# First norm's modulation in pieces of 128 columns, x turned by diagonal matmuls, and a 23rd weight slot that the second gate uses later

## The chip, the cores and the metric

The kernel runs on one core of a Trainium2 chip. The metric is the device time of one execution in microseconds (us). The core has a matmul engine (TensorE, "PE" in the profile, whose weight loads are listed apart as "PEld"), two elementwise engines (VectorE, "DVE", and ScalarE, "ACT"), GpSimd ("POOL"), a queue engine ("SP") and 16 DMA engines. Each engine works through its own list of instructions in the order of the program. Engines wait for one another through semaphores. TensorE's clock has two levels, and the profile shows which was granted (1.00 is 2.4 GHz, 0.50 is 1.2 GHz).

## The reference

One transformer block on 256 tokens of width 1024, everything in float32. What matters here:

```
mod = silu(c) @ w_ada + b_ada                     # 6 x 1024
sh1, sc1, ga1, sh2, sc2, ga2 = split(mod)
h = rms_norm(x, g_norm1) * (1 + sc1) + sh1
z = h @ w_in                                      # q, k, v, conv parts, gates
merged = gate_a * (attention @ w_pa) + gate_b * (conv @ w_pb)
x = x + ga1 * (merged @ w_o)
h2 = rms_norm(x, g_norm2) * (1 + sc2) + sh2
x = x + ga2 * moe(h2)      # top group of 4, top 2 of 8 experts, 32 experts, SwiGLU, width 512
```

## The kernel before

All weights pass once through the core, about 257 MB, as one stream of DMAs of 1 MB (768 KB for the pieces of q, k, v), laid out on the host in the order of use. `stream` lists them: first the 54 pieces of `FRONT` (w_ada, w_in, w_pa, w_pb, w_o), then for each of 8 groups of four experts 16 pieces of w1 and w3 and 8 of w2, 192 in all. A piece goes into a slot (1 MB of SBUF). `pump` issues the next piece from SP whenever a slot is free, and `release`, called where a piece was last read, frees its slot and calls `pump`. Slots and order are settled when the program is built; on the chip SP waits at each issue for the semaphore that says that the slot's last reader is done, and for its eighth DMA back to have landed. There are 12 slots at first, two more lent by the gate buffers, and as buffers of the front are given up `more_slots` adds 3 (`late`), 4 (`late2`) and 3 (`late3`), while the lent ones go: 22 slots in the expert stage.

**The front** is a list of units. A unit takes 512 columns of a weight, splits them into a high and a low part (ACT L396 and DVE or POOL L397, up to four units ahead), and does three fp32r matmuls for each product on PE (L428). There are 24 units for q, k, v (three for each of 8 row blocks k), 56 for the other columns of w_in, 16 for w_pa and w_pb, and 16 for w_o. Other work is put between units as tasks: `after(i, g)` starts task g behind unit i, and each `yield n` lets n units pass.

**The first norm's modulation** must be there before the units of row block k: `hpart(0, k)` and `hpart(1, k)` (high and low part of h, transposed) are made by `modulate1(k)` from hf (x, normed and transposed), a1 (1 + scale, times g_norm1) and sh1. The scale and the shift come as four pieces of 256 columns each, two row blocks to a piece, in the order of the list `FIRST`. A piece is summed over its 1024 rows either by 8 matmuls of 32x256 on PE (L516) followed by two small ones that turn the row into columns (L501), or, for the scale pieces 2 and 3, by 8 operations on DVE (L331, L333) and the same two small matmuls. At the start x is multiplied by its 1/rms (DVE L360, ACT L361) and turned by 16 PE transposes (L365). The copies L372 and L374 bring it back to SBUF as hf.

**The second gate** ga2 is summed in the front into bank B[0] (`gate2_task`, L773). It is copied to `ysb` after the front, and finished between the first group's `up` and `down` with its bias row, which ACT loads at L937.

**The end of the front.** After the last unit of w_o the residual, the squares, the transposes and the router's logits (L844) follow, then a chain of small DVE operations picks the experts up to the one-hot `ohs` (L980). PE ranks the tokens (L982 to L984), DVE makes the gather matrices Gt and Wt (L1016, L1018), PE gathers tokens with `gather` (L1027), DVE and ACT modulate them with `modulate2`, and `up(0)` begins its matmuls (L1060). Nothing of the expert weights is released before that. `warm(n)` is n matmuls of ident by ident (L267) whose result nobody reads; they only keep PE busy.

## Time and profile before

| | us |
|---|---|
| median of 3 runs | 663.52 (663.48 to 663.66) |
| the profiled execution | 665.23 |
| its span, first to last instruction | 663.5 |
| PE busy | 533.8 |
| DVE busy | 195.5 |
| ACT busy | 146.7 |

Busy times are sums over stages with different limits, and PE's ends are modelled, so a PE that waits inside a run of matmuls can be shown as busy. HBM reads are 257.12 MB, 389 GB/s over the span. The chain that ended last has 34% of the span in DMA and 3% in PE; it is followed back only as far as 410.71 us.

### The profile page before, as it was taken

Reading aid. Unit: us, or ns where it says so; the run is one execution under the profiler, and the core shown is the slowest. Engines: PE = TensorE matmul, PEld = TensorE weight load, DVE = VectorE, ACT = ScalarE, POOL = GpSimd, SP = SyncE. Lnnn points to the kernel's source line nnn. Section 1 sums busy time; section 2 is a strip of 40 time slices with the busy share of each in tenths; the row PEclk is TensorE's granted clock in tenths of the full one; section 3 lists DMA queues with packets and bytes.
Section 4 is the critical chain, followed back from the end, with each engine's and each line's share of the span. In section 5 each row is a group of like instructions: output and inputs, shape, how many; then the busy total and the mean of one; then the engine's idle time right before and its main releaser. Section 6 shows DMA issues by size and latency. Waiting matters only on the chain. (4 is left out here: it accounts for less than half of the span.)

```text
span 663.5 us, 11736 instructions
## 1 busy us (share of the span) xinstructions
PE 533.8 (80%) x5054; PEld 322.1 (49%) x5055; DVE 195.5 (29%) x405; ACT 146.7 (22%) x290; POOL 40.9 (6%) x59
## 2 busy tenths in 40 slices
PE   7999999999999899988575756676766875677765
PEld 6678897988998637363043104301510540161033
DVE  4687449657896412020020001001100100010002
ACT  4536456744555220010010001000000100010001
POOL 0012511500040000000000000000000000000000
PEclk9999999999999898999888799968987596897669
DMA  8999994699959699999999997999999999999996
GB/s 315 426 425 398 426 421 154 244 356 378 399 199 407 282 410 426 425 427 424 428 427 423 423 426 328 423 428 427 425 426 426 428 426 425 428 425 425 427 427 255
DMA packets 37765, 259.01 MB, mean 390 GB/s; under 512 B 4545, under 2 KB 5673, under 8 KB 7242
## 3 DMA queue, kind: packets, MB, share of 16 engines
q1 hardware_dynamic: 36136, 256.98, 93.4%
q10 hardware_dynamic: 1362, 1.05, 0.5%
q8 instruction: 42, 0.69, 0.4%
q0 software_dynamic: 208, 0.15, 0.1%
q14 instruction: 17, 0.14, 0.1%
HBM read 257.12 MB, written 1.05 MB: 389 GB/s over the span
## 5 line engine op out<-in xcount | busy, mean ns | idle before, releaser
L1060 PE MATMUL ps<-slot,xg 128*32 128x512 f32 x1024 | 163.4, 745 | 76.4 <-DMA slot<-in_up_dram 71.4
L1060 PEld LDWEIGHTS ps<-slot,xg 128*32 128x32 f32 x1024 | 26.1, 120 | 197.8 <-DMA slot<-in_up_dram 160.3
L428 PE MATMUL ps<-hbuf,sthi 128*128 128x256 f32 x512 | 94.8, 287 | 0.0
L428 PEld LDWEIGHTS ps<-hbuf,sthi 128*128 128x128 f32 x512 | 79.0, 190 | 11.4 <-ACT sthi L396 6.7
L397 DVE TENSOR_TENSOR stlo<-slot,sthi 128x512 fp32r<-128x512 f32 x100 | 72.0, 723 | 37.9 <-ACT sthi L396 36.7
L396 ACT ACTIVATE sthi<-slot 128x512 fp32r<-128x512 f32 x108 | 68.0, 630 | 62.7 <-PE ps L428 50.2
L1068 DVE TENSOR_TENSOR sl<-sl,ps 128x512 f32<-128x512 f32 x8 | 5.5, 688 | 254.7 <-PE ps L1060 246.4
L1080 PE MATMUL ps<-slot,sl 128*32 128x128 f32 x2048 | 67.9, 287 | 14.6 <-DMA slot<-in_down_dram 9.7
L428 PE MATMUL ps<-hbuf,stlo 128*128 128x256 f32 x256 | 72.2, 282 | 0.7 <-POOL stlo L397 0.7
L1080 PEld LDWEIGHTS ps<-slot,sl 128*32 128x32 f32 x2048 | 57.1, 115 | 29.1 <-DMA slot<-in_down_dram 13.3
L1047 ACT ACTIVATE GW<-ps 128x256 f32<-128x256 f32 x8 | 3.1, 384 | 239.1 <-PE ps L1046 239.1
L1088 PE MATMUL ps<-ysb,GW 128*128 128x512 f32 (+1 forms) x76 | 37.1, 615 | 17.6 <-DVE ysb L1086 17.6
L428 PEld LDWEIGHTS ps<-hbuf,stlo 128*128 128x128 f32 x256 | 48.5, 190 | 0.9 <-POOL stlo L397 0.9
L428 PE MATMUL ps<-sthi,hbuf 128*128 128x512 f32 x128 | 43.2, 404 | 1.1 <-ACT hbuf L528 0.9
L1086 DVE TENSOR_TENSOR ysb<-ps,ga 128x512 f32<-128x512 f32 (+1 forms) x19 | 11.5, 606 | 90.7 <-PE ps L1080 83.7
L1027 PEld LDWEIGHTS ps<-GW,x 128*128 128x128 f32 x256 | 33.4, 212 | 6.4 <-issue 5.6
L1027 PE MATMUL ps<-GW,x 128*128 128x128 f32 x256 | 36.0, 302 | 0.2 <-DVE GW L1018 0.2
L1088 PEld LDWEIGHTS ps<-ysb,GW 128*128 128x128 f32 x76 | 13.3, 203 | 30.9 <-DVE ysb L1086 22.1
L428 PEld LDWEIGHTS ps<-sthi,hbuf 128*128 128x128 f32 x128 | 23.7, 188 | 8.9 <-issue 1.6
L1033 ACT ACTIVATE xg<-ps,sm,sm 128x128 f32<-128x128 f32 x32 | 12.4, 457 | 59.8 <-PE ps L1027 59.8
L428 PE MATMUL ps<-stlo,hbuf 128*128 128x512 f32 x64 | 25.1, 392 | 0.0
L1035 DVE TENSOR_SCALAR xg<-ps,sm,sm 128x128 f32<-128x128 f32 x32 | 11.2, 404 | 35.0 <-PE ps L1027 35.0
(264 smaller groups left out, 429.2 us busy)
## 6 DMA issues: line engine op xcount, KB each, us to landing
slot<-in_up_dram SPq DMA_DIRECT2D x128, 1024.0 KB, 19.6
slot<-in_down_dram SPq DMA_DIRECT2D x64, 1024.0 KB, 19.6
slot<-in_front_dram SPq DMA_DIRECT2D x42, 1024.0 KB, 11.4
slot<-in_front_dram SPq DMA_DIRECT2D x8, 768.0 KB, 14.4
gates<-in_front_dram SPq DMA_DIRECT2D x4, 1024.0 KB, 7.0
x<-in_x_dram SPq DMA_DIRECT2D x2, 512.0 KB, 3.7
out_dram<-x ACTq DMA_DIRECT2D x1, 512.0 KB
out_dram<-x ACTq DMA_DIRECT2D x4, 128.0 KB, 1.8
```

The source lines that it names most:

```text
L396: S.activation(hi, src, AF.Copy)
L397: (G if i in on_pool else V).tensor_sub(lo, src, hi.bitcast(F32))
L428: PE.matmul(o, l, r, start=start and n == 0, stop=stop and n == 2, skip_group_check=True)
L1027: PE.matmul(o[:, 128 * (k % 4):128 * (k % 4) + 128], x[:, t, 128 * k:128 * k + 128], Gt[:, t, :], start=t == 0, stop=t == 1)
L1033: S.activation(xg[:, k, :], src, AF.Identity, bias=sh2[:, k:k + 1], scale=a2[:, k:k + 1])
L1035: V.tensor_scalar(xg[:, k, :], src, a2[:, k:k + 1], sh2[:, k:k + 1], op0=OP.mult, op1=OP.add)
L1047: S.activation(WT.rearrange("p t n -> p (t n)"), YC[:, :256], AF.Copy)
L1060: PE.matmul(o[js, :], xg[:, k, js], w[:, j, :], start=k == 0, stop=k == DK - 1)
L1068: V.tensor_mul(sl, sl, HB)
L1080: PE.matmul(bank[js, cs], hidT[:, k, js], w[:, 4 * j + k, :], start=k == 0, stop=k == 3, skip_group_check=True)
L1086: V.tensor_mul(ysb[:, cs], (bank or (YC, YD)[n])[:, cs], ga2[:, ns])
L1088: PE.matmul(ACC[t][n][:, cs], WT[:, t, :], ysb[:, cs], start=q == 0, stop=q == NQ - 1, skip_group_check=True)
```

## The change

- `FIRST` goes. The scale and the shift now come as 8 pieces `mod1.i` of 1 MB, each with the 128 scale and the 128 shift columns of row block i, in turn with `qkv.i`. Every piece is summed on PE (8 matmuls of 32x256), copied by DVE, turned by two small matmuls, and a1 and sh1 of that block are made by one DVE operation each. Task i starts behind unit 3i - 3.
- c, b_ada and g_norm1 are loaded from ACT's queue instead of SP's. x is now first on SP, and four pieces follow it before the other small loads.
- x is not scaled first: two diagonal matrices (ident times 1/rms) are made, and `x_turn(b)` does x times diagonal as ordinary matmuls, four to a bank.
- `late3` has 4 slots instead of 3: 23 in all, until the piece w3.0.7 is used up. Its slot is then kept (`kept`) and holds ga2 and ysb.
- The bias row of ga2 is loaded by ACT into misc in the front, and added in bank B[0] by two matmuls with one row, ahead of the first sums of `gate2_task`, which starts two units earlier and lets two units pass. The copy of B[0] to ysb moves behind `up(0)`.
- Around the router: `squares(1, 1)` and the sums for 1/rms move up; `warm(8)` becomes `warm(26)`, `warm(4)` becomes `warm(9)`; two blocks of tokens instead of three are gathered before the first matmuls of `up(0)`; the transposes of Wt come one step later.

```diff
-    for nm in FIRST:
-        i = int(nm[2:])
-        if nm[0] == "q":
-            f.append((f"qkv.{i}", "w_in", 128 * i, 1, 0, 1536))
-        else:
-            f.append((f"{nm[:2]}1.{i}", "w_ada", 0, 8, 512 * (SC1 if nm[:2] == "sc" else SH1) + 256 * i, 256))
+    for i in range(DK):
+        f.append((f"mod1.{i}", "mod1", 0, 8, 256 * i, 256))
+        f.append((f"qkv.{i}", "w_in", 128 * i, 1, 0, 1536))
...
     def release(key):
-        free.append(where.pop(key))
+        i = where.pop(key)
+        if key == LAST_UP:
+            kept.append(i)
+            return
+        free.append(i)
         pump()
...
-    load_rows("c", SY)
+    load_rows("c", S)
+    load_rows("b_ada", S)
+    load_rows("g_norm1", S)
...
-    load_rows("b_ada", SY)
-    load_rows("g_norm1", SY)
-    pump(1)
+    pump(4)
     for nm in ("g_norm2", "conv_w", "conv_b"):
         load_rows(nm, SY)
-    pump(2)
...
-    xh = [flat(sq), flat(vt)]
-    V.tensor_scalar(xh[0], x[:, 0, :], rinv1[:, 0:1], None, op0=OP.mult)
-    S.activation(xh[1], x[:, 1, :], AF.Copy, scale=rinv1[:, 1:2])
-
-    def x_transposes(t):
-        for k in range(DK):
-            PE.transpose(PS[k // 2][:, 256 * (k % 2) + 128 * t:256 * (k % 2) + 128 * t + 128],
-                         xh[t][:, 128 * k:128 * k + 128], ident)
-
-    def x_copies():
...
+    dg = flat(sq)[:, :256].rearrange("p (t n) -> p t n", t=2)
+    for t in range(2):
+        V.tensor_scalar(dg[:, t], ident, rinv1[:, t:t + 1], None, op0=OP.mult)
+
+    def x_turn(b):
+
+        for k in (2 * b, 2 * b + 1):
+            for t in range(2):
+                PE.matmul(PS[b][:, 256 * (k % 2) + 128 * t:256 * (k % 2) + 128 * t + 128],
+                          x[:, t, 128 * k:128 * k + 128], dg[:, t], start=True, stop=True)
+        d = flat(hf[:, 2 * b:2 * b + 2, :])
+        if b % 2:
+            S.activation(d, PS[b], AF.Copy)
+        else:
+            V.tensor_copy(d, PS[b])
...
-    def first_ada(i, shift, bank):
-
-        key = f"{('sc', 'sh')[shift]}1.{i}"
-        w = cols256(slot(key))
+    ab1 = small([128, 8])
+
+    def first_bias():
+
+        V.scalar_tensor_tensor(ab1, col("b_ada", 4 * SC1, 8), 1.0, col("g_norm1", 0, 8), op0=OP.add, op1=OP.mult)
+
+    def first_ada(i):
+
+        bank = B[6 + i % 2]
+        w = cols256(slot(f"mod1.{i}"))
         for kk in range(2):
             for j in range(4):
-                k = 2 * j + kk
+                k = 4 * kk + j
                 PE.matmul(bank[32 * j:32 * j + 32, :256], sil[:, k:k + 1].to_broadcast([128, 32]), w[:, k, :],
                           start=kk == 0, stop=kk == 1)
-        release(key)
-        p = part[shift][:, :256]
-        if shift and not i:
-            V.tensor_copy(p, bank[:, :256])
-        else:
-            S.activation(p, bank[:, :256], AF.Copy)
-        yield 1
-        first_cols(i, shift, bank, p, sel)
+        release(f"mod1.{i}")
+        p = part[i % 2][:, :256]
+        V.tensor_copy(p, bank[:, :256])
+        yield 1
+        for c in range(2):
+            PE.matmul(bank[:, c:c + 1], p[:, 128 * c:128 * c + 128], sel, start=True, stop=True)
+        V.scalar_tensor_tensor(a1[:, i:i + 1], bank[:, 0:1], col("g_norm1", i, 1), ab1[:, i:i + 1], op0=OP.mult,
+                               op1=OP.add)
+        V.tensor_add(sh1[:, i:i + 1], bank[:, 1:2], col("b_ada", 4 * SH1 + i, 1))
+
+    def first_task(i):
+        yield from first_ada(i)
+        modulate1(i)
...
-    def first_scale(i):
-
...
-        p = misc[:, 256 * i:256 * i + 256]
-        w = cols256(slot(f"sc1.{i}"))
-        for k in range(DK):
-            ada_sum(p, w[:, k, :], k, k == 0)
-            if k % 2:
-                yield 1
-        release(f"sc1.{i}")
-        first_cols(i, 0, B[6], p, one)
-
-    def first_shift(i):
-
-        yield from first_ada(i, 1, B[7])
-        for k in (2 * i, 2 * i + 1):
-            modulate1(k)
-            yield 1
...
     def gate2_task(bank):
 
+        row = misc[0:1, :D]
+        S.dma_start(row, dram("b_ada", 512 * GA2, [[D, 1], [1, D]]))
+        yield 2
+        for half in range(2):
+            PE.matmul(bank[64 * half:64 * half + 32, :], one[0:1, :].to_broadcast([1, 32]),
+                      row[:, 512 * half:512 * half + 512], start=True, stop=False, skip_group_check=True)
         for i in range(4):
             for kk in range(2):
                 for half in range(2):
-                    quarter_sum(f"ga2.{i}", 2 * i + kk, 2 * kk + half, 2 * half + kk, bank, i == 0, i == 3)
+                    quarter_sum(f"ga2.{i}", 2 * i + kk, 2 * kk + half, 2 * half + kk, bank, i == 0 and kk == 1, i == 3)
             release(f"ga2.{i}")
             yield 3
...
-    for i in range(1, 4):
-        after(6 * i - 6, lambda i=i: first_scale(i))
-        after(6 * i - 3, lambda i=i: first_shift(i))
+    for i in range(1, DK):
+        after(3 * i - 3, lambda i=i: first_task(i))
...
-    after(63, lambda: gate2_task(B[0]))
+    after(61, lambda: gate2_task(B[0]))
...
-    a, b = first_ada(0, 0, B[6]), first_ada(0, 1, B[7])
+    first = first_ada(0)
     columns("a", B[4])
-    next(a)
-    x_transposes(0)
-    next(a, 0)
-    x_transposes(1)
-    x_copies()
-    next(b)
-    warm(4)
-    next(b, 0)
-    for k in range(2):
-        split_next()
-        modulate1(k)
-    run_units(19)
+    first_bias()
+    x_turn(0)
+    next(first)
+    for b in range(1, 4):
+        x_turn(b)
+    split_next()
+    next(first, 0)
+    modulate1(0)
+    run_units(20)
...
-    more_slots(late3, 3)
+    more_slots(late3, 4)
...
-    ysb = late3.tile([128, 512], F32, name="ysb")
...
-    ga2 = late3.tile([128, D], F32, name="ga2")
     small_pool[0] = late3
-    S.dma_start(ga2[0:1, :], dram("b_ada", 512 * GA2, [[D, 1], [1, D]]))
...
     resid(1, 1)
     for t in range(2):
         logits(0, t)
+    squares(1, 1)
+    ms2, rinv2, nu2 = small([128, 2]), small([128, 2]), small([128, 2])
+    V.tensor_add(ms2, ss2[:, :, 0], ss2[:, :, 1])
+    V.tensor_scalar(ms2, ms2, 1.0 / D, EPS, op0=OP.mult, op1=OP.add)
     transp(1, 0)
-    squares(1, 1)
+    S.activation(rinv2, ms2, AF.Sqrt)
     transp(1, 1)
     for t in range(2):
         logits(1, t)
-    S.activation(ysb, B[0], AF.Copy)
-    warm(8, B[4])
-
-    ms2, rinv2, nu2 = small([128, 2]), small([128, 2]), small([128, 2])
-    V.tensor_add(ms2, ss2[:, :, 0], ss2[:, :, 1])
-    V.tensor_scalar(ms2, ms2, 1.0 / D, EPS, op0=OP.mult, op1=OP.add)
-    S.activation(rinv2, ms2, AF.Sqrt)
+    warm(26, B[4])
...
-    warm(4, B[4])
+    warm(9, B[4])
...
             if q == 0:
 
-                for kk in range(min(k + 2, DK) if k else 0, min(k + 3, DK)):
+                for kk in range(k + 1 if k else 0, min(k + 2, DK)):
...
-            if k == (6 if q == 0 else 4):
+            if k == (7 if q == 0 else 4):
                 weights_T(q)
...
     for q in range(NQ):
         up(q)
         if q == 0:
+            room = flat(slots[kept[0]])
+            ga2, ysb = room[:, :D], room[:, D:D + 512]
+            S.activation(ysb, B[0], AF.Copy)
             for half in range(2):
-                g = ga2[:, 512 * half:512 * half + 512]
-                PE.matmul((HA, HB)[half], sel2[:, half:half + 1].to_broadcast([128, 128]), ysb, start=True, stop=False)
-                PE.matmul((HA, HB)[half], one[0:1, :].to_broadcast([1, 128]), g[0:1, :], start=False, stop=True)
-                V.tensor_copy(g, (HA, HB)[half])
+                PE.matmul((HA, HB)[half], sel2[:, half:half + 1].to_broadcast([128, 128]), ysb, start=True, stop=True)
+                V.tensor_copy(ga2[:, 512 * half:512 * half + 512], (HA, HB)[half])
...
+    w["mod1"] = np.stack([w["w_ada"][:, 512 * b:512 * b + D].reshape(D, DK, 128) for b in (SC1, SH1)], 2).reshape(D, -1)
```

In PE's list at the end of the front, from the clock matmuls behind the router's logits to the first expert matmuls (ps_74 and ps_73 are the bank that nobody reads, sm_2222 and sm_2244 the one-hots `ohs`, GW the gather matrices, and a slot with xg an expert matmul), before:

```order
L267 MATMUL ps_74<-ident 128x128 x8
L982 LDWEIGHTS before
L982 MATMUL ps_73<-sm_2222,before 128x32
L983 LDWEIGHTS ones
L983 MATMUL ps_73<-sm_2222,ones 128x32
L984 LDWEIGHTS before
L984 MATMUL ps_73<-sm_2222,before 128x32
L267 MATMUL ps_74<-ident 128x128 x4
L1027 MATMUL ps_76<-GW,x 128x128 x2
L1027 MATMUL ps_77<-GW,x 128x128 x2
L1027 MATMUL ps_76<-GW,x 128x128 x2
L1060 MATMUL ps_74<-slot_1526,xg 32x512 x4
```

and now:

```order
L265 MATMUL ps_73<-ident 128x128 x26
L957 LDWEIGHTS before
L957 MATMUL ps_72<-sm_2244,before 128x32
L958 LDWEIGHTS ones
L958 MATMUL ps_72<-sm_2244,ones 128x32
L959 LDWEIGHTS before
L959 MATMUL ps_72<-sm_2244,before 128x32
L265 MATMUL ps_73<-ident 128x128 x9
L1002 MATMUL ps_75<-GW,x 128x128 x2
L1002 MATMUL ps_76<-GW,x 128x128 x2
L1035 MATMUL ps_73<-slot_1532,xg 32x512 x4
```

The ranking matmuls stand behind 26 clock matmuls instead of 8, the gathers behind 9 instead of 4, and the expert matmuls behind two gathered blocks instead of three.

In DVE's list at the start, from the end of 1/rms to the modulation of the first row block (ps_70 to ps_73 are the banks with x turned, gates_114 is hf, sm_221 is a1, sm_222 is sh1, stlo and sthi are the parts of the first unit's weights), before:

```order
L323 SCALAR_TENSOR_TENSOR sm_227<-sm_228,sm_227 128x2
L360 TENSOR_SCALAR sq<-x,sm_227 128x1024
L257 COPY cols_a<-ps_74 128x56
L506 TENSOR_TENSOR sm_221<-ps_76,cols_a 128x2
L507 SCALAR_TENSOR_TENSOR sm_221<-sm_221,cols_a 128x2
L374 COPY gates_114<-ps_70 128x512
L374 COPY gates_114<-ps_72 128x512
L521 COPY part_220<-ps_77 128x256
L504 TENSOR_TENSOR sm_222<-ps_77,cols_a 128x2
L397 TENSOR_TENSOR stlo_105<-slot_79,sthi_101 128x512
L529 TENSOR_SCALAR gates_114<-gates_114,sm_221,sm_222 128x256
L530 TENSOR_TENSOR hbuf_99<-gates_114,hbuf_99 128x256
```

and now (hf is gates_113, a1 is sm_220, sh1 is sm_221, the banks are ps_69 to ps_72):

```order
L321 SCALAR_TENSOR_TENSOR sm_226<-sm_227,sm_226 128x2
L359 TENSOR_SCALAR sq<-ident,sm_226 128x128 x2
L255 COPY cols_a<-ps_73 128x56
L500 SCALAR_TENSOR_TENSOR sm_238<-cols_a 128x8
L371 COPY gates_113<-ps_69 128x512
L513 COPY part_218<-ps_75 128x256
L371 COPY gates_113<-ps_71 128x512
L394 TENSOR_TENSOR stlo_104<-slot_77,sthi_100 128x512
L517 SCALAR_TENSOR_TENSOR sm_220<-ps_75,cols_a,sm_238 128x1
L519 TENSOR_TENSOR sm_221<-ps_75,cols_a 128x1
L527 TENSOR_SCALAR gates_113<-gates_113,sm_220,sm_221 128x256
L528 TENSOR_TENSOR hbuf_98<-gates_113,hbuf_98 128x256
```

a1 and sh1 of the first row block, which the modulation waits for, now stand behind the split L394 of the first unit's weights; before, L397 stood behind them.

## Rows read from the trace of the kernel before

**Rows 1.** The page, the span in 40 slices of 16.6 us: DMA's rate.

```profile
GB/s 315 426 425 398 426 421 154 244 356 378 399 199 407 282 410 426 425 427 424 428 427 423 423 426 328 423 428 427 425 426 426 428 426 425 428 425 425 427 427 255
```

**Rows 2.** Waits of PE, 24 to 205 us: waited for, us in total, times, longest.

```profile
PE ps L773 <- DVE sq L642: 1.0, 1, 1.0
PE ps L428 <- POOL stlo L397: 0.7, 1, 0.7
```

**Rows 3.** Timeline of the start: start, us, engine, line, output<-input, count, idle before.

```profile
0.78 0.41 SPq L224 DMA_DIRECT2D qkb<-in_c_dram  x1
1.24 0.83 SPq L229 DMA_DIRECT2D x<-in_x_dram  x2
...
8.56 0.16 DVE L323 SCALAR_TENSOR_TENSOR sm<-sm,sm 128x2 f32<-128x2 f32 x1
...
11.04 1.09 PE L365 MATMUL ps<-ident,sq 128*128 128x128 f32 x8
...
15.49 0.63 ACT L396 ACTIVATE sthi<-slot 128x512 fp32r<-128x512 f32 x1 [1.39 <-DMA slot<-in_front_dram]
...
15.87 0.16 DVE L504 TENSOR_TENSOR sm<-ps,cols_a 128x2 f32<-128x2 f32 x1 [0.95 <-PE ps L501]
16.06 0.60 ACT L528 ACTIVATE hbuf<-gates,sm,sm 128x256 fp32r<-128x256 f32 x1
16.15 0.69 DVE L397 TENSOR_TENSOR stlo<-slot,sthi 128x512 fp32r<-128x512 f32 x1
...
16.72 0.50 PE L428 MATMUL ps<-sthi,hbuf 128*128 128x512 f32 x1 [0.89 <-ACT hbuf L528]
```

**Rows 4.** Timeline of PE among the units of q, k, v, around 27 and 46 us.

```profile
26.89 0.39 PE L428 MATMUL ps<-sthi,hbuf 128*128 128x512 f32 x1
27.12 0.50 PE L501 MATMUL ps<-sel,part 128*128 128x1 f32 x4
27.48 0.48 PE L428 MATMUL ps<-sthi,hbuf 128*128 128x512 f32 x1
...
45.79 0.40 PE L428 MATMUL ps<-sthi,hbuf 128*128 128x512 f32 x1
46.11 1.07 PE L516 MATMUL ps<-gates,sm 128*32 128x256 f32 x16
47.11 0.50 PE L428 MATMUL ps<-sthi,hbuf 128*128 128x512 f32 x1
```

**Rows 5.** Timeline where the second gate's sums begin, and the issue of its bias row.

```profile
133.01 0.60 ACT L694 ACTIVATE qkb<-ps 128x512 f32<-128x512 f32 x1 [2.01 <-PE ps L691]
...
136.44 1.06 PE L773 MATMUL ps<-slot,sm 128*32 128x512 f32 x8
...
215.10 0.52 ACTq L937 DMA_DIRECT2D ga<-in_b_ada_dram  x1
```

**Rows 6.** Waits of SP's queue, 210 to 232 us.

```profile
SPq L137 <- DMA ga<-in_b_ada_dram: 4.2, 1, 4.2
```

**Rows 7.** Timeline from the router's last logits to the first expert matmuls.

```profile
219.01 2.03 PE L267 MATMUL ps<-ident 128*128 128x128 f32 x16
...
222.41 0.23 DVE L980 TENSOR_TENSOR sm<-sm 128x64 bf16<-128x64 f32 x1
222.69 0.18 PE L982 MATMUL ps<-sm,before 128*128 128x32 bf16 x1 [1.64 <-DVE sm L980]
...
223.66 0.42 DVE L1018 TENSOR_TENSOR GW<-GW,sm 128x256 f32<-128x256 f32 x1
224.14 2.48 PEld L1027 LDWEIGHTS ps<-GW,x 128*128 128x128 f32 x12 [0.43 <-DVE GW L1018]
...
226.84 2.36 PE L1060 MATMUL ps<-slot,xg 128*32 128x512 f32 x16
...
229.13 0.71 PE L1027 MATMUL ps<-GW,x 128*128 128x128 f32 x4
```

**Rows 8.** Timeline of SP: the two issues after its longest wait.

```profile
228.41 1.35 SPq L137 DMA_DIRECT2D slot<-in_down_dram  x2
```

**Rows 9.** Windows around that wait: us, busy of PE, PEld, DVE, ACT, POOL, granted clock, DMA share, GB/s.

```profile
223.00:224.00 1.00, 0.90 (x8) 0.71 (x7) 0.93 (x3) 0.00 (x0) 0.00 (x0) 1.00 1.09 459
225.00:226.00 1.00, 1.00 (x6) 1.00 (x6) 0.41 (x1) 0.00 (x0) 0.00 (x0) 0.50 0.06 25
230.00:231.00 1.00, 1.00 (x12) 0.26 (x8) 0.00 (x0) 0.98 (x2) 0.00 (x0) 1.00 0.97 369
```

More of the change, by code (lines that the diff above doesn't have):

```diff
@@ L39 @@
 QI, KI, VI, XBI, BGI, CGI, GI = 0, 1, 2, 3, 4, 5, 6
-FIRST = ("sc0 sh0 qk0 sc1 qk1 sh1 qk2 sc2 qk3 sh2 qk4 sc3 qk5 sh3 qk6 qk7").split()
 REST = ("in00 in01 in10 m20 m21 in11 m22 m23 in20 in21 in30 m24 m25 m26 in31 m27 in40 g100 in41 g101 g20 in50 g21 "
@@ L81 @@
 FRONT = _front()
+LAST_UP = "w3.0.7"
 LENT = ("mod2.7", "ga2.1")
@@ L95, in block_kernel @@
     ctx.enter_context(tc.manual_schedule())
-    const.tile([128, 8], F32, name="fill")
     def dram(name, off, ap):
@@ L112, in block_kernel @@
     sent = [0]
+    kept = []
     def cols256(s):
@@ L358, in block_kernel @@
     rsqrt_tail(rinv1, nu, ms)
-    xh = [flat(sq), flat(vt)]
-    V.tensor_scalar(xh[0], x[:, 0, :], rinv1[:, 0:1], None, op0=OP.mult)
-    S.activation(xh[1], x[:, 1, :], AF.Copy, scale=rinv1[:, 1:2])
-    def x_transposes(t):
-        for k in range(DK):
-            PE.transpose(PS[k // 2][:, 256 * (k % 2) + 128 * t:256 * (k % 2) + 128 * t + 128],
-                         xh[t][:, 128 * k:128 * k + 128], ident)
-    def x_copies():
-        for b in range(4):
-            d = flat(hf[:, 2 * b:2 * b + 2, :])
-            if b % 2:
-                S.activation(d, PS[b], AF.Copy)
-            else:
-                V.tensor_copy(d, PS[b])
+    dg = flat(sq)[:, :256].rearrange("p (t n) -> p t n", t=2)
[11 more added lines that the diff above has]
+            V.tensor_copy(d, PS[b])
     units = []
@@ L496, in block_kernel @@
             wo_unit(n, k, [B[b] for b in wob[n]])
-    def first_cols(i, shift, bank, p, w):
-        for c in range(2):
-            PE.matmul(bank[:, c:c + 1], p[:, 128 * c:128 * c + 128], w, start=True, stop=True)
-        cs = slice(2 * i, 2 * i + 2)
-        if shift:
-            V.tensor_add(sh1[:, cs], bank[:, :2], col("b_ada", 4 * SH1 + 2 * i, 2))
-        else:
-            V.tensor_add(a1[:, cs], bank[:, :2], col("b_ada", 4 * SC1 + 2 * i, 2))
-            V.scalar_tensor_tensor(a1[:, cs], a1[:, cs], 1.0, col("g_norm1", 2 * i, 2), op0=OP.add, op1=OP.mult)
-    def first_ada(i, shift, bank):
-        key = f"{('sc', 'sh')[shift]}1.{i}"
-        w = cols256(slot(key))
+    ab1 = small([128, 8])
[4 more added lines that the diff above has]
+        w = cols256(slot(f"mod1.{i}"))
         for kk in range(2):
             for j in range(4):
-                k = 2 * j + kk
+                k = 4 * kk + j
                 PE.matmul(bank[32 * j:32 * j + 32, :256], sil[:, k:k + 1].to_broadcast([128, 32]), w[:, k, :],
                           start=kk == 0, stop=kk == 1)
-        release(key)
-        p = part[shift][:, :256]
-        if shift and not i:
-            V.tensor_copy(p, bank[:, :256])
-        else:
-            S.activation(p, bank[:, :256], AF.Copy)
-        yield 1
-        first_cols(i, shift, bank, p, sel)
+        release(f"mod1.{i}")
+        p = part[i % 2][:, :256]
+        V.tensor_copy(p, bank[:, :256])
+        yield 1
+        for c in range(2):
[6 more added lines that the diff above has]
+        modulate1(i)
     def modulate1(k):
@@ L530, in modulate1 @@
         V.tensor_sub(hpart(1, k), hf[:, k, :], hpart(0, k).bitcast(F32))
-    def first_scale(i):
-        if i == 1:
-            yield from first_ada(i, 0, B[6])
-            return
-        p = misc[:, 256 * i:256 * i + 256]
-        w = cols256(slot(f"sc1.{i}"))
-        for k in range(DK):
-            ada_sum(p, w[:, k, :], k, k == 0)
-            if k % 2:
-                yield 1
-        release(f"sc1.{i}")
-        first_cols(i, 0, B[6], p, one)
-    def first_shift(i):
-        yield from first_ada(i, 1, B[7])
-        for k in (2 * i, 2 * i + 1):
-            modulate1(k)
-            yield 1
     ssq = small([128, 2, 2, NH])
```

## The prediction

> **What bounds the kernel now.** I read the slices of the page first. From the sixteenth slice of 40 on DMA moves about 425 GB/s almost throughout (the dip in slice 25 shifts with the rest), so the expert stage lives on its stream [rows 1]. Before that there are two dips: slices 7 to 12, and slice 14, where the front ends. In the first the stream waits for slots, that is for PE. The waits of PE say the same: between 24 and 205 us it waited twice, 1.0 and 0.7 us, both times for another engine and never for a weight [rows 2]. So the front is a row of PE work, and a microsecond added to PE there moves everything behind it by a microsecond. What hides nothing there is PE's own list; DVE's and ACT's work is free as long as PE does not wait for it.
>
> The second dip is the joint between the stages. The stream fills its 22 slots and stops; in the window at 225 us it moves 25 GB/s, at 230 us 369 [rows 9]. SP issues again at 228.41, when the first expert piece is released [rows 8], 1.57 us after the first expert matmul began at 226.84 [rows 7]. From there to the end the stream never has slack to give back. The time is therefore: when PE ends the front, plus how long the router takes to the first release, plus the pieces that are then not yet loaded, 2.45 us each (1.049 MB at 427 GB/s, [rows 1]).
>
> **The change, part by part.** Three places count: the start, the units of q, k, v with the second gate's bias, and the joint.
>
> *Start.* x is issued at 1.24 [rows 3]; now it is the first on SP, where c was at 0.78, so 0.46 earlier, and 1/rms is there at 8.26 instead of 8.72 (L323 begins at 8.56). The matmuls that turn x are new. A transpose of 128x128 left one record, and eight took 1.09 us [rows 3]; an ordinary fp32 matmul of ident by ident leaves two (16 records for `warm(8)`, [rows 7]). So the 16 turns take about 32 x 0.11 = 3.5 us where the transposes took 1.8, in one row with the first piece's sums (1.0): PE is through at 8.55 + 4.5 = 13.05 plus the small ones, 13.4. Now the order of DVE decides. ACT copies the last bank (0.55) and then makes the high part of the first unit (0.63, [rows 3]), to 14.5; DVE's low part (0.69) stands ahead of a1 and sh1, to 15.3; these two take 0.2 each with the handover (15.87 to 16.06), and L528 0.60. The first unit can start at 16.3 against 16.72, and I take -0.5. Bounds: -1.5 if copies and splits overlap better, +0.3 if c or b_ada come late beside x.
>
> *Units of q, k, v.* A unit's matmuls start 0.23 apart (26.89 to 27.12). With the sums of a piece between them, 45.79 to 47.11 is 1.32, so a piece costs 1.09 us of PE; the two small matmuls cost 27.48 - 26.89 - 0.23 = 0.36 [rows 4]. Before, PE summed six pieces of eight: two ahead of the first unit, four among the units (DVE had the other two, for nothing, beside PE). Now it is one ahead and seven among: three more, **+3.3**. The small matmuls are seven pairs among the units instead of six: **+0.4**. Then a wait: a row block's a1 and sh1 are now made one after the other behind the same small matmuls, where before only the shift was left (16.06 - 15.87 = 0.19 later each time). What is late next is the low part of h, the third matmul of the unit that begins the block, and PE's list is queued behind it. In the trace of before that low part comes just in time, so I count 7 x 0.19 = **+1.3**; with slack it is nothing, and 1.6 if each waits longer.
>
> *Bias of the second gate.* Two more matmuls of 512 columns ahead of the first sums. L773's eight records, four matmuls on four parts of the array, took 1.06 [rows 5]; two take two passes as well: **+0.9**. The row for them is issued by ACT behind the copy L694 at 133.01 + 0.60, so near 133.7, and PE is there at 136.44, 2.7 us later [rows 5]. The only like transfer, the same 4 KB row at L937, was issued at 215.10, and SP waited 4.2 us for it, which is when it landed [rows 5, 6]. By that row PE waits 1.6 us; below it is nothing, since 215 us was a time of full stream. I take the middle, **+0.6**. The Trainium skill ("DMA: Bandwidth & Descriptors", Anatomy of one DMA) has a fixed cost of about 2.0 us for a small DMA and holds most of it for the receipt; by that the row would be there before PE, this term 0.9 in all and the sum 0.6 less. The trace's 4.2 us differs from it, and it decides.
>
> *Joint.* The 23rd slot lets the stream load one piece more before it stops: **-2.45**, if the release is not later. It is. `warm(8)` is 16 records in 2.03 us from 219.01, and behind it PE waited 1.64 us for the one-hots, to 222.69 [rows 7]. The 26 now are 52 records, at (2.03 - 0.28) / 15 = 0.117 each 6.1 us, to 225.1; at the 0.11 of the transposes to 224.8. The ranking stands behind them, 2.1 to 2.4 later. DVE needs 223.66 + 0.42 - 222.69 = 1.4 after that, the nine clock matmuls 2.0 to 2.1, so the gathers begin near 227.1 instead of 224.14. What is won back is the clock: it was 0.50, 1.2 GHz, in the window at 225 [rows 9], after PE had stood still, and the twelve records of gathers took 2.70 to the first expert matmul. At full clock four take 0.71 [rows 7], so two blocks and the 0.41 of the modulation come to 1.3. The first expert matmul is then at 228.4, and the first release 1.1 later instead of 1.57: about 229.4, 1.0 later than before. So the joint gives -2.45 + 1.0 = **-1.5** (bounds -2.5 and -0.5). The Trainium skill ("TensorE: Matmul & The Clock Gate", Step-by-step) says that only weight loads are pulled ahead and matmuls keep program order; the rows agree, L982's matmul ran behind all of `warm(8)`, and without the rule the joint would give the -4.4 of the second rival.
>
> The copy of ysb behind `up(0)` holds PE for about 0.6 us at some 246 us; there the pieces lie ready in the slots and PE is ahead of the stream's need, so nothing.
>
> **Sum:** -0.5 + 3.3 + 0.4 + 1.3 + 0.9 + 0.6 - 1.5 = +4.5 us. The profiled span of 663.5 becomes 668.0 (its own time 665.23 becomes 669.7). The median of the runs, 663.52, is as long as the span, so I predict **668.0 us** for the median.
>
> **The rivals.** First, *faster: the start follows the stream, not PE.* Only 1.75 MB instead of 2.75 MB of pieces stand ahead of the first unit's end, one megabyte less, 2.45 us. For it: ACT waited 1.39 us for the first unit's weights [rows 3]. If the units then ran at the stream's pace (1.75 MB a block are 4.3 us), the added sums would hide in it: -2.45 + 1.5 - 1.5 = -2.5, 661.0. It decides if three units and their sums take less than 4.3 us; [rows 4] give 3 x 1.39 + 1.09 + 0.36 = 5.6. Against it also: no wait for weights in [rows 2]. Chance 0.09.
>
> Second, *the clock matmuls hold nothing up.* If 26 of them take no more than the 3.7 us that the choice of experts takes, the ranking stays at 222.69, all behind it is at full clock, and the first release comes near 226.5, before the stream stops at all: joint -4.4, time 665.1. It needs 0.07 us a record; none in the trace is that short. Chance 0.12.
>
> Third, *the slot gives nothing*: the release comes 2.4 us later, because the gathers wait for more than I see. Joint 0, time 669.5. Chance 0.11.
>
> Fourth, *no difference*: PE has hidden slack in the front, its ends being modelled, and the added work fits in. Then only start, bias and joint are left, -0.5 + 1.5 - 1.5, 663.0. Chance 0.06.
>
> **How the numbers follow.** The forecast has 0.62, with its own range 666.0 to 670.0 from the bounds of start, wait, row and joint (they will not all fall on one side). For 8 in 10 the range goes down to 663.8, which takes in the second rival, and up to 670.4, which takes in the third; the first and the fourth, 0.15, stay below it. Changes under 0.2% (1.3 us) can't be told from none here. Slower: the forecast, the third rival and half of the second, 0.79. Same: the rest of the second and most of the fourth, 0.11. Faster: the first and a rest of the fourth, 0.10.
>
> **What would show it.** In the profile after: the first L425 matmul near 16.3 and the last unit of q, k, v about 4.5 us later than before; L509 in eight blocks of about 1.0; short PE waits for DVE's hbuf at the start of each row block; a PE wait for a DMA ahead of L780; 52 records of L265 with the ranking directly behind them and no wait for ohs; clock 1.00 through the first expert matmuls; and a gap in the stream of some 4 us instead of 5. The prediction is wrong if the units of q, k, v end no later than before, or if the ranking still waits for DVE.

## The result

The changed kernel takes **671.74 us** (median of 4, 669.64 to 672.81) against 663.59 (663.48 to 663.99): the ratio is 1.0118, 95% interval 1.0100 to 1.0135. So it is 8.15 us slower, where 4.5 were predicted. The profiled execution took 671.93 us, its span is 670.2.

The direction came from where the prediction had it: PE's row in the front. The timeline of before and of the changed kernel, at the first of the 56 units behind those of q, k, v (called feature units below), at the last matmul of w_o and at SP's issues of the last eight pieces:

```profile
59.40 0.40 PE L428 MATMUL ps<-hbuf,sthi 128*128 128x256 f32 x2
213.94 0.40 PE L428 MATMUL ps<-sthi,hbuf 128*128 128x512 f32 x1
619.62 19.95 SPq L137 DMA_DIRECT2D slot<-in_down_dram  x8
```

```profile
66.71 0.40 PE L425 MATMUL ps<-hbuf,sthi 128*128 128x256 f32 x2
224.01 0.40 PE L425 MATMUL ps<-sthi,hbuf 128*128 128x512 f32 x1
627.57 19.84 SPq L132 DMA_DIRECT2D slot<-in_down_dram  x8
```

PE ends the front 10.07 us later, where +6.0 was predicted, and at its end the stream is 8.0 us late. The 2.1 between the two is what the joint gave back (predicted 1.5). The spans of these two executions differ by 6.7 only: from ACT's last operation to the end it took 4.1 us in the one of before, and 2.8 to 2.9 in the changed kernel and in every run below, so the stream's 8.0 is what to set beside the 8.15 of the medians.

The page of the changed kernel, DMA's rate in 40 slices (of before: [rows 1]), and the waits of PE from 24 to 225 us ([rows 2]):

```profile
GB/s 345 409 427 423 396 357 111 266 210 351 427 297 265 425 337 427 423 426 424 428 426 426 422 426 371 386 426 426 427 425 427 427 424 428 426 426 428 425 426 285
```

```profile
PE ps L780 <- DMA misc<-in_b_ada_dram: 1.7, 1, 1.7
PE ps L750 <- DVE sq L619: 1.0, 1, 1.0
PE ps L425 <- POOL stlo L394: 0.7, 1, 0.7
PE ps L254 <- DVE sm L519: 0.4, 1, 0.4
```

The two waits of before are still there, and the bias row has added the longest. The short waits at each row block's start are under what this view lists.

The timeline of the start ([rows 3]; L265 are clock matmuls, L365 turns x, L509 sums a piece, L425 are the units):

```profile
2.46 6.64 PE L265 MATMUL ps<-ident 128*128 128x128 f32 x32
...
8.34 0.48 DVE L359 TENSOR_SCALAR sq<-ident,sm 128x128 f32<-128x128 f32 x2
...
9.22 1.16 PE L365 MATMUL ps<-sq,x 128*128 128x128 f32 x8
...
10.31 1.07 PE L509 MATMUL ps<-gates,sm 128*32 128x256 f32 x16
...
11.31 2.94 PE L365 MATMUL ps<-sq,x 128*128 128x128 f32 x24
...
16.43 0.60 ACT L526 ACTIVATE hbuf<-gates,sm,sm 128x256 fp32r<-128x256 f32 x1 [0.96 <-DVE sm L519]
...
17.08 0.50 PE L425 MATMUL ps<-sthi,hbuf 128*128 128x512 f32 x1 [2.48 <-ACT hbuf L526]
...
19.51 1.93 PE L509 MATMUL ps<-slot,sm 128*32 128x256 f32 x16
```

The diagonals are there by 8.82, but PE comes to turn x at 9.22: the 32 clock records of the start fill its list until then. The first unit begins at 17.08, behind a standstill of PE of 2.48 us. Then eight matmuls of sums take 1.93 us, where they took 1.07 at 10.31. The windows show why (the number before the last two is the granted clock):

```profile
18.00:19.00 1.00, 1.00 (x4) 0.77 (x4) 1.00 (x2) 0.59 (x2) 0.00 (x0) 0.80 0.99 381
19.00:20.00 1.00, 1.00 (x10) 0.26 (x12) 0.74 (x2) 0.32 (x1) 0.00 (x0) 0.50 0.93 367
20.00:21.00 1.00, 1.00 (x16) 0.33 (x8) 0.00 (x0) 0.31 (x1) 0.00 (x0) 0.50 1.06 442
21.00:22.00 1.00, 1.00 (x9) 0.53 (x3) 0.46 (x2) 0.00 (x0) 0.00 (x0) 0.50 1.01 424
```

The clock was at its lower level, 1.2 GHz, from about 18.6 to 22 us, after PE had stood still. The kernel before has `warm(4)` at this place.

The timeline where the second gate's bias is added ([rows 5, 6]):

```profile
140.82 0.23 ACTq L777 DMA_DIRECT2D misc<-in_b_ada_dram  x1
...
145.49 1.05 PE L780 MATMUL ps<-misc,one 1*32 1x512 f32 x4 [1.69 <-DMA misc<-in_b_ada_dram]
146.47 1.06 PE L750 MATMUL ps<-slot,sm 128*32 128x512 f32 x8
147.47 0.51 PE L425 MATMUL ps<-hbuf,sthi 128*128 128x256 f32 x2
```

The row took 4.7 us from its issue until PE went on, and the two bias matmuls took 0.98.

The joint, by timeline ([rows 7, 8]) and by windows ([rows 9]):

```profile
229.08 6.05 PE L265 MATMUL ps<-ident 128*128 128x128 f32 x52
...
232.39 0.22 DVE L955 TENSOR_TENSOR sm<-sm 128x64 bf16<-128x64 f32 x1
...
234.97 0.18 PE L957 MATMUL ps<-sm,before 128*128 128x32 bf16 x1
...
238.25 1.92 PE L1035 MATMUL ps<-slot,xg 128*32 128x512 f32 x16
```

```profile
239.38 0.33 SPq L132 DMA_DIRECT2D slot<-in_down_dram  x1
```

```profile
236.00:238.00 2.00, 2.00 (x20) 2.00 (x18) 0.59 (x2) 0.00 (x0) 0.00 (x0) 1.00 0.81 344
238.00:240.00 2.00, 1.94 (x18) 0.42 (x16) 0.20 (x1) 0.46 (x1) 0.00 (x0) 1.00 0.01 4
240.00:242.00 2.00, 2.00 (x20) 0.94 (x20) 0.56 (x3) 0.00 (x0) 0.00 (x0) 1.00 0.78 213
```

The one-hots are ready at 232.61, the ranking begins at 234.97 behind the last clock record. The clock stays at 1.00, and the first release comes 1.13 us behind the first expert matmul. The release comes 15.37 us behind the last unit (14.47 before), 0.9 more. The stream stops later by its extra piece and stands for about 2.9 us instead of 5.2 (the idle shares of half-microsecond windows, added up).

### The profile page after: what moved, and what is told of

The parts are those of the page before. It is cut to its first block, busy times and chain, and to the rows that moved or that the text cites. A ratio compares the mean times of both kernels' runs of the same rounds, so it can differ in the third digit from the quotient of the medians.

```text
span 670.2 us, 11909 instructions
## 1 busy us (share of the span) xinstructions
PE 546.0 (81%) x5140; PEld 330.1 (49%) x5141; DVE 191.7 (29%) x402; ACT 144.5 (22%) x284; POOL 41.4 (6%) x59
## 4 chain that ended last, share of the span: by engine, by line
DMA 49%; PE 28%; DVE 1%; ACT 1%; issue 0%; POOL 0%; SPq 0%; DVEq 0%; ACTq 0%
DMA slot<-in_up_dram 32%; DMA slot<-in_down_dram 16%; PE ps L425 10%; PE ps L1035 5%; PE ps L1055 3%; PE ps L1002 3%; PE ps L1063 1%; PE ps L265 1%; DMA misc<-in_b_ada_dram 1%; PE ps L750 1%; PE ps L1152 1%; PE ps L1180 1%; DVE slot L1061 0%; PE ps L1045 0%; DVE sl L1043 0%
## 5 line engine op out<-in xcount | busy, mean ns | idle before, releaser
L1035 PE MATMUL ps<-slot,xg 128*32 128x512 f32 x1024 | 159.0, 730 | 68.5 <-DMA slot<-in_up_dram 64.9
L425 PE MATMUL ps<-hbuf,sthi 128*128 128x256 f32 x512 | 94.7, 286 | 0.0
L1055 PE MATMUL ps<-slot,sl 128*32 128x128 f32 x2048 | 69.9, 289 | 19.5 <-DMA slot<-in_down_dram 14.5
L425 PEld LDWEIGHTS ps<-hbuf,sthi 128*128 128x128 f32 x512 | 79.0, 190 | 11.4 <-ACT sthi L393 6.7
L394 DVE TENSOR_TENSOR stlo<-slot,sthi 128x512 fp32r<-128x512 f32 x97 | 68.5, 715 | 40.4 <-ACT sthi L393 39.7
L393 ACT ACTIVATE sthi<-slot 128x512 fp32r<-128x512 f32 x105 | 66.0, 630 | 61.4 <-PE ps L425 51.1
L425 PE MATMUL ps<-hbuf,stlo 128*128 128x256 f32 x256 | 72.1, 282 | 0.7 <-POOL stlo L394 0.7
L1063 PE MATMUL ps<-slot,GW 128*128 128x512 f32 (+1 forms) x76 | 41.0, 670 | 13.4 <-DVE slot L1061 13.4
L425 PEld LDWEIGHTS ps<-hbuf,stlo 128*128 128x128 f32 x256 | 48.5, 190 | 0.9 <-POOL stlo L394 0.9
L425 PE MATMUL ps<-sthi,hbuf 128*128 128x512 f32 x128 | 45.4, 414 | 2.7 <-ACT hbuf L526 2.5
L1061 DVE TENSOR_TENSOR slot<-ps,slot 128x512 f32<-128x512 f32 (+1 forms) x19 | 11.5, 606 | 91.8 <-PE ps L1055 91.8
L1002 PEld LDWEIGHTS ps<-GW,x 128*128 128x128 f32 x256 | 31.5, 202 | 6.8 <-issue 6.4
L425 PEld LDWEIGHTS ps<-sthi,hbuf 128*128 128x128 f32 x128 | 23.7, 190 | 13.3 <-issue 3.3
L1063 PEld LDWEIGHTS ps<-slot,GW 128*128 128x128 f32 x76 | 14.4, 219 | 28.4 <-DVE slot L1061 18.2
L425 PE MATMUL ps<-stlo,hbuf 128*128 128x512 f32 x64 | 25.4, 396 | 0.0
L1042 ACT ACTIVATE sl<-ps 128x512 f32<-128x512 f32 x8 | 4.8, 597 | 74.6 <-PE ps L1035 74.6
```

The costliest lines, as they stand in the source:

```text
L393: S.activation(hi, src, AF.Copy)
L394: (G if i in on_pool else V).tensor_sub(lo, src, hi.bitcast(F32))
L425: PE.matmul(o, l, r, start=start and n == 0, stop=stop and n == 2, skip_group_check=True)
L1002: PE.matmul(o[:, 128 * (k % 4):128 * (k % 4) + 128], x[:, t, 128 * k:128 * k + 128], Gt[:, t, :], start=t == 0, stop=t == 1)
L1035: PE.matmul(o[js, :], xg[:, k, js], w[:, j, :], start=k == 0, stop=k == DK - 1)
L1055: PE.matmul(bank[js, cs], hidT[:, k, js], w[:, 4 * j + k, :], start=k == 0, stop=k == 3, skip_group_check=True)
```

## The experiments

Theory: the front is PE's row, so each wait and each matmul in it counts in full, and the miss lies in terms that were left out or sized too small: the start, the clock, the row, the joint's clock matmuls. Rival: the stream or the slots took the time, and edits on PE give nothing. Medians are in us; those of the kernel before beside the same runs were 663.2 to 663.7.

**Clock matmuls at the start.**

```diff
     next(first, 0)
+    warm(10)
     modulate1(0)
```

> The changed kernel with ten clock matmuls behind the first piece's two small matmuls, where PE stood still for 2.48 us until 17.08. Theory (the clock fell to its lower level, 0.50 from 18.5 to 22 us, because PE had stood still there): the granted clock stays at 1.00, the second block of sums takes 1.05 again instead of 1.91, and the second unit begins about 3.0 us behind the first instead of 4.29, so the front ends 1.2 us earlier and the kernel takes about 670.5 us against 671.7. Rival (the clock falls there whatever PE did before, or the start hides in the stream): the second block still takes 1.9, or the front ends no earlier, 671.7 us.

Measured 670.26 (ratio 1.0103, 1.0078 to 1.0128). The timeline of PE:

```profile
13.81 2.48 PE L265 MATMUL ps<-ident 128*128 128x128 f32 x20
16.44 0.50 PE L425 MATMUL ps<-sthi,hbuf 128*128 128x512 f32 x1
...
18.47 1.07 PE L509 MATMUL ps<-slot,sm 128*32 128x256 f32 x16
19.47 0.50 PE L425 MATMUL ps<-sthi,hbuf 128*128 128x512 f32 x1
```

The granted clock is 1.00 there, the sums take 1.07 instead of 1.93, and the second unit begins 3.03 behind the first. From first unit to first feature unit it is 48.02 us instead of 49.63, so the clock cost 1.6. The standstill is what matters: six profiled executions had it and no clock matmuls, and all six fell to 0.50 behind it; three with clock matmuls there did not. The profiled execution gave part of it back by chance: it waited 1.54 us for the bias row, and here the clock fell behind that wait too (0.50 in 146 to 148 us).

**Bias matmuls behind the second piece.**

```diff
-        for half in range(2):
-            PE.matmul(bank[64 * half:64 * half + 32, :], one[0:1, :].to_broadcast([1, 32]),
-                      row[:, 512 * half:512 * half + 512], start=True, stop=False, skip_group_check=True)
         for i in range(4):
+            if i == 2:
+                for half in range(2):
+                    PE.matmul(bank[64 * half:64 * half + 32, :], one[0:1, :].to_broadcast([1, 32]),
+                              row[:, 512 * half:512 * half + 512], start=False, stop=False, skip_group_check=True)
```

> The changed kernel with the second gate's two bias matmuls moved behind the second of its four pieces; the row is loaded at the same place. Theory (PE's row is serial and it waited 1.69 us for the row alone): no wait for the row, the two bias matmuls still cost 1.0, from the last feature unit ahead of the bias to the next 3.5 us or less instead of 5.25, everything behind it 1.7 us earlier, about 670.0 us. Rival (the row only came last; behind it PE would have waited for the piece, or the stream gives the time back): the wait turns into one for a slot, or the end does not move, 671.7 us.

Measured 670.20 (1.0097, 1.0078 to 1.0116). No wait for the row is left, and from first feature unit to the last matmul of w_o it is 155.52 us instead of 157.30: 1.78 less. Before it was 154.54; the 1.0 that remains are the two bias matmuls.

**Fewer clock matmuls ahead of the ranking** (`warm(26)` to `warm(13)`).

> The changed kernel with 13 clock matmuls instead of 26 ahead of the ranking. Theory (the 52 records held the ranking from 232.6, when DVE had the one-hots, to 234.9): the ranking begins as soon as the one-hots are there, the first release comes 2.2 us earlier and the stream stops for less than 1 us instead of 2.6, so 669.5 us. Rival A (without them the clock falls as in the kernel before, 0.50 for some 3 us): the gathers and the first expert matmuls take 1 to 2 us longer and give most of it back, 671 to 672 us. Rival B (the joint gave only what the 23rd slot holds, and the release does not count): no difference, 671.7 us.

Measured 669.56 (1.0088, 1.0066 to 1.0110). The first release comes 13.07 us behind the last unit instead of 15.37, with the clock at 1.00 throughout: 2.3 earlier, where the theory had 2.2.

**Sums one unit earlier.**

```diff
-        after(3 * i - 3, lambda i=i: first_task(i))
+        after(max(3 * i - 4, 0), lambda i=i: first_task(i))
```

> The changed kernel with each row block's sums begun one unit earlier, so that its modulation is one unit ahead of its use. Theory (the third and second matmul of each row block waited for DVE's low part, 0.25 us a block in seven blocks): the pair 0.35 and 0.34 at the start of a block becomes 0.23 and 0.23 in six of them, 1.5 us off the front, 670.2 us. Rival A (the 0.1 is the price of another shape of matmul, not a wait): it stays, 671.7 us. Rival B (a piece is then not there yet): PE waits for a slot, slower than 671.7 us.

Measured 668.46 (1.0085, 1.0054 to 1.0115). PE's timeline at the start of a row block, the changed kernel and then this one:

```profile
31.28 0.39 PE L425 MATMUL ps<-stlo,hbuf 128*128 128x512 f32 x1
31.63 0.73 PE L425 MATMUL ps<-sthi,hbuf 128*128 128x512 f32 x2
32.19 0.39 PE L425 MATMUL ps<-stlo,hbuf 128*128 128x512 f32 x1
```

```profile
29.09 0.39 PE L425 MATMUL ps<-stlo,hbuf 128*128 128x512 f32 x1
29.32 0.62 PE L425 MATMUL ps<-sthi,hbuf 128*128 128x512 f32 x2
29.78 0.39 PE L425 MATMUL ps<-stlo,hbuf 128*128 128x512 f32 x1
```

0.35 and 0.56 for one and two matmuls became 0.23 and 0.46. It was a wait for DVE's low part of h: in the changed kernel DVE makes that part from 31.15 to 31.58, and the weight load behind the first matmul waits for it:

```profile
31.62 0.30 PEld L425 LDWEIGHTS ps<-sthi,hbuf 128*128 128x128 f32 x2 [0.39 <-DVE hbuf L528]
```

The units of q, k, v take 47.88 us instead of 49.63, 1.75 less, near the theory's 1.5. But the median fell by 3.3, twice what the theory said. In the trace the rest is a first unit that began 0.6 earlier and a wait for the row that was 0.9 shorter; neither is shown to come from the edit, and both vary among the other executions.

**All four together.**

> The changed kernel with all four edits of the first experiments: clock matmuls at the start, the bias matmuls later, 13 clock matmuls ahead of the ranking, each row block's sums one unit earlier. Theory (the four terms add: 1.3, 1.7, 2.2 and 1.6): about 664.9 us, that is 1.3 us over the kernel before, what the three more pieces on PE cost less the joint. Rival (they overlap, since the stream takes over as the bound of the front once PE is faster): 667 us or more.

Measured 664.49 (1.0025, 1.0012 to 1.0038): 7.25 of the 8.15 are gone, where the theory's four terms add up to 6.8 and the four single runs, by their medians, to 8.5. From first unit to first feature unit it is 46.36 us.

**The joint alone, on the front of before; then with 13 clock matmuls; then with 13 and 6.** These have the diff's parts on slots, joint and second gate, with the bias matmuls behind the second piece.

```diff
-    more_slots(late3, 3)
+    more_slots(late3, 4)
...
-    warm(8, B[4])
+    warm(26, B[4])
...
-    warm(4, B[4])
+    warm(9, B[4])
```

> The kernel before with the change's joint alone: the 23rd slot, 26 and 9 clock matmuls, two gathered blocks, the square sum ahead of the second transposes, and the second gate's bias in its sums (its two matmuls behind the second piece, so that nothing waits for the row); start and units of q, k, v stay those of before. Theory (the joint gives 2.0 to 2.3 us by itself, the front is what costs; the bias matmuls cost 1.0): about 662.4 us against 663.6. Rival (the joint gained only because the longer front left the stream more time to fill the slots): 664.6 us.

Measured 663.18 (0.9997, 0.9988 to 1.0007).

> The same with 13 clock matmuls ahead of the ranking instead of 26. Theory (every microsecond by which the ranking begins earlier comes off the end, as long as the stream stops at the joint): another 2.2 us, about 660.2 us. Rival (with the shorter front the stream has fewer pieces loaded, so the earlier release is given back as waiting for pieces, or the clock falls): 662.4 us or more.

Measured **660.67 (0.9964, 0.9953 to 0.9976)**: faster than both kernels, and 2.5 under the run with 26.

> The kernel before with the change's joint, 13 clock matmuls ahead of the ranking and 6 instead of 9 ahead of the gathers; the second gate's row is loaded in the front, as in the run with 13 and 9. Theory (the 0.7 us by which the gathers came earlier with a late row is a gain by itself): 0.6 us under the 660.7 of 13 and 9, 660.0 us. Rival (the stream is not stopped long enough for it to count): 660.7 us.

Measured 660.76 (0.9957, 0.9941 to 0.9972). The release did come 0.62 earlier behind the last unit (12.45 against 13.07), but the end did not move. Where it is given back is not settled: the trace, in which the stream ran at 270 to 344 GB/s for 3 us from 231 on (401 to 442 in the run with 9), is of the slowest of six executions (662.51).

The joint alone missed its 1.2 us. The next run bears on the reason: the kernel before has a joint that varies.

**Two more pieces on PE, in the kernel before.**

```diff
     def first_scale(i):
-        if i == 1:
+        if i:
             yield from first_ada(i, 0, B[6])
             return
```

> The kernel before, with the two pieces that DVE summed (scale of the third and fourth pair of row blocks) summed by PE like the others. Theory (a piece's sums stand in PE's row with nothing to hide them: 1.05 and twice 0.1 for the change of shape): 2.5 us slower, 665.8 us. Rival (PE has hidden slack there, or DVE's share held something up): 663.3 us.

Measured 665.16 (1.0027, 1.0014 to 1.0040). From first unit to first feature unit it is 45.20 us against 42.68, so +2.52, the theory's number; the median rose by 1.7 (0.9 to 2.7). Its joint is that of before, and so is PE's wait for the one-hots. The timeline and the windows ([rows 7, 9]), with the gathers of before in the first line:

```profile
224.14 2.77 PE L1027 MATMUL ps<-GW,x 128*128 128x128 f32 x12 [0.24 <-DVE GW L1018]
```

```profile
225.14 0.18 PE L982 MATMUL ps<-sm,before 128*128 128x32 bf16 x1 [1.63 <-DVE sm L980]
...
226.59 1.93 PE L1027 MATMUL ps<-GW,x 128*128 128x128 f32 x12 [0.24 <-DVE GW L1018]
228.45 1.92 PE L1060 MATMUL ps<-slot,xg 128*32 128x512 f32 x16
```

```profile
227.00:230.00 3.00, 2.94 (x27) 1.50 (x26) 0.82 (x2) 0.46 (x1) 0.00 (x0) 1.00 0.03 14
```

Behind the same wait (1.63, before 1.64) the clock stayed at 1.00, the gathers took 1.93 instead of 2.77, and the release came 13.18 behind the last unit instead of 14.47. So the low clock at the joint, from which the prediction credited the change with a gain, belonged to that execution of before and does not come each time.

**Two pieces back to DVE, in the changed kernel.**

```diff
+    ON_DVE = (2, 5)
...
+        for k in range(DK):
+            ada_sum(p, w[:, k, :], k, k == 0)
...
-        after(3 * i - 3, lambda i=i: first_task(i))
+        after(3 * i - (6 if i in ON_DVE else 3), lambda i=i: first_task(i))
```

> The changed kernel with the pieces of row blocks 2 and 5 summed by DVE, eight operations each, as the kernel before had it for two of its pieces, begun three units earlier. Theory (a piece's sums cost PE 1.05 and twice 0.1 around them, and DVE has room beside PE): two pieces less, 2.5 us, about 669.2 us. Rival (DVE makes the low parts of the weights too, and eight more operations make these late, or wait for a piece that is not there yet): PE waits for stlo or hbuf, 671.7 us or more.

Measured 675.96 (1.0190, 1.0164 to 1.0217): the rival's time, but not its wait. Waits of PE, 10 to 225 us:

```profile
PE ps L520 <- DVE misc L331: 2.8, 2, 1.4
```

The rival had PE waiting for stlo or hbuf; what it waited for were the two sums themselves. DVE finished each 1.4 us after PE came to its small matmuls. In the trace the units of q, k, v take 0.8 us more than in the changed kernel, and 1.3 more went behind the wait for the row, where the clock fell. That execution (674.04) is 2.1 over the changed kernel's; the rest of the median's 4.2 is not explained, and nothing about the price of a piece follows from this run.

**Fewer clock matmuls at the very start, then the start in another order as well.**

```diff
-    warm(16)
+    warm(12)
```

> The changed kernel with 12 instead of 16 clock matmuls at the very start (24 records instead of 32). Theory (the matmuls that turn x stand behind these on PE; where their pace stays at 0.21 a record until 8.4 us they end at 9.1, after the diagonals are there at 8.6, and the first unit is late by just that): they end by 7.6, x is turned from 8.6 on, the first unit begins near 16.4 instead of 17.08, about 671.0 us. Rival (PE then stands still ahead of the turning, the clock is low for it, and the turning takes longer): first unit at 17 us or later, 671.7 us or more.

Measured 671.63 (1.0128, 1.0106 to 1.0150): the median can't tell it from the changed kernel. In the trace PE turned x from 8.71 on and the first unit began at 16.57, as said; the clock fell behind the standstill as before, and again behind the row.

```diff
     next(first, 0)
+    warm(8)
     modulate1(0)
+    split_next()
...
-    warm(9, B[4])
+    warm(6, B[4])
```

> The changed kernel with the four edits, 12 clock matmuls at the very start, the first block's modulation ahead of the first split, and 6 clock matmuls ahead of the gathers. Theory (low and high part of the first weights, 0.69 on DVE and 0.62 on ACT, stood ahead of the first modulation; start 0.7, gathers 0.6): first unit near 16.2, 663.2 us, no slower than the kernel before. Rival (the start is bound by something else): 664.5 us.

Measured 663.42 (1.0006, 0.9994 to 1.0018). This has the four edits and 12 clock matmuls at the very start as well. The first unit begins at 15.71, 1.2 us earlier than with the four edits alone, and the median is 1.1 lower. The last matmul of w_o comes 1.0 earlier (217.81 against 218.82), so the start alone can account for it.

**The bias out of the front.**

```diff
-        S.dma_start(row, dram("b_ada", 512 * GA2, [[D, 1], [1, D]]))
...
         up(q)
         if q == 0:
+            S.dma_start(ga2[0:1, :], dram("b_ada", 512 * GA2, [[D, 1], [1, D]]))
...
+        if q == 0:
+            S.activation(ysb, B[0], AF.Copy)
...
+                PE.matmul((HA, HB)[half], one[0:1, :].to_broadcast([1, 128]), g[0:1, :], start=False, stop=True)
+                V.tensor_copy(g, (HA, HB)[half])
         combine(q, 0)
```

> The kernel before with the change's joint, 13 clock matmuls ahead of the ranking, and the second gate's bias out of the front: its row goes into the kept slot after the first group's up matmuls and is added ahead of the first combine. Theory (its two matmuls cost 1.0 us of the front, and in the first group PE has time): 1.0 us under the 660.7 of the same kernel with the bias in the front, 659.7 us. Rival (the first group is where the stream needs its slots back, so that PE's extra work there stops the stream): 660.7 us or more.

Measured 663.84 (1.0017, 1.0005 to 1.0029), 3.2 slower than with the bias in the front. PE was not the cause. Waits of SP from 226 to 262 us, the timeline, and windows:

```profile
SPq L139 <- PE ps L1062: 15.5, 7, 10.8
SPq L139 <- DMA slot<-in_b_ada_dram: 14.7, 1, 14.7
```

```profile
248.89 0.52 ACTq L1177 DMA_DIRECT2D slot<-in_b_ada_dram  x1
...
250.35 6.73 SPq L139 DMA_DIRECT2D slot<-in_up_dram  x9
```

```profile
248.00:250.00 2.00, 1.31 (x32) 1.07 (x36) 1.03 (x3) 0.60 (x1) 0.00 (x0) 1.00 0.45 186
250.00:252.00 2.00, 2.00 (x19) 1.65 (x12) 0.00 (x0) 0.00 (x0) 0.00 (x0) 0.51 0.34 61
```

SP's list holds a wait for the row's landing in the midst of the stream's issues. ACT, with the first group's work ahead of it, issued the row at 248.89 only; SP issued nothing from 235.6 to 250.35, and the stream ran dry. The row itself was quick here, 1.5 us from its issue until SP went on.

> The same with 6 instead of 9 clock matmuls between ranking and gathers. Theory (their 18 records end 0.7 us after DVE has made the one-hot matrix at 224.4): the gathers begin 0.6 us earlier behind the ranking, the first release too, 659.1 us. Rival (the stream hardly stops any more, or what releases the next piece is the pace of the expert matmuls): no difference to the former, 659.7 us.

Measured 663.03 (1.0004, 0.9992 to 1.0016), 0.8 under the former, with the same wait of SP (14.6 us).

## Why the prediction was wrong

By its own steps, with the two profiled executions:

- **Start: the step that failed.** -0.5 was predicted, +0.36 came, and 1.6 us of low clock behind it were not in the sum at all. The chain of DVE and ACT was followed, with PE free to turn x at 8.55. But in PE's list the turning stands behind the 32 clock records, which before ended at 7.95 with 2 us to spare, and here at 9.1. Seven profiled executions of the new start with 32 records have their first unit 8.26 us behind the last record's start in six, from 16.52 to 18.34; in the seventh (last record at 7.38) it waited for the diagonals and began at 16.44, near the 16.3 predicted. A part of that spread comes from c, which ACT's queue now loads: in four of the nine executions of the new start it let PE begin at 3.18 to 3.55 instead of 2.3, and in none of the seven with c on SP's queue (2.30 to 2.48); the prediction bounded the term at +0.3 for a late c, and why c is late is not shown. And the diff took `warm(4)` out of a standstill that had grown to 2.48 us (0.89 before).
- **Pieces: right.** +3.7 for three pieces and a pair of small matmuls. With all four edits there are neither the waits nor the low clock, and it takes 46.36 us from first unit to first feature unit where the front of before takes 42.63 (13 clock matmuls): 3.73.
- **Waits for a1 and sh1: a little small.** +1.3 predicted; at full clock it is 46.36 without them (all four edits) and 48.02 with them (clock matmuls at the start): 1.66.
- **Bias matmuls: right** (0.9; 0.98). **Row: mis-sized.** 0.6 was taken between 0 and 1.6, but 1.69 came. The like row said 4.2 us, and the new one took 4.7. The middle was chosen against the measurement at hand. It was also not the only one: the DMA view of before lists two rows of b_ada of 2 KB, loaded by GpSimd's queue beside the stream (at 36.5 and 50.5 us), with 5.2 us from issue to landing. The Trainium skill ("DMA: Bandwidth & Descriptors", Anatomy of one DMA) has a fixed cost of about 2.0 us, for DMAs that GpSimd issues; no run here shows so little under a full stream.
- **Joint: right in these two traces** (release 0.9 later, 1.0 predicted; one piece more). But a part of the gain was the low clock of before's one profiled execution: against a joint without it (13.18) the new one (15.37 less 2.45) gains 0.3 instead of 1.6. The joint alone, -0.1 by the medians with 1.0 of bias matmuls in it, gained 1.1, which lies between the two, as it would if the kernel before loses the clock there in some executions only; how often it does is not shown.
- The sum by what was measured, start, clock, pieces, waits, bias, row and joint: 0.4 + 1.6 + 3.7 + 1.7 + 1.0 + 1.7 - 2.1 = 8.0. Of the 3.5 over the predicted 4.5, the start and its clock are 2.5 and the row 1.1.

Of the rivals none decided. The expected signs did show: 52 records with the ranking right behind them, no wait for the one-hots, and a wait for a DMA ahead of L780. Those that did not: the first unit came at 17.08 instead of 16.3, the units of q, k, v ended 7.3 us later instead of 4.5, one block of sums took 1.93, and the stream stood for 2.9 us instead of 4.

## What to carry on

When new work is put into an engine's list, look at what already stands ahead of it there: clock matmuls that cost nothing while the engine waits anyway are a queue for whatever stops waiting. Where the nearest row for a cost lies at one end of the bounds, take it rather than the middle. Clock matmuls should end when the data behind them is ready and not later: 13 instead of 26, with the same extra slot, turned a joint that, with its bias matmuls, gained nothing into one that gains 2.6 us.
